# Layout of the query planes in DRAM, and their loads and stores, in the wide attention units of an encoder layer

## Chip, cores, metric

One core of one Trainium2 chip. The metric is the device time of one execution in microseconds; the median of three runs of the kernel before is 2199.79 us (2197.37 to 2203.7).

## The reference

One encoder layer is applied to two sequences with the same weights, A of 1024 positions (x_prompt) and B of 512 (x_sample). After an RMS norm one projection gives the inputs of an mLSTM branch, of a dilated window attention and of gates; both branches are projected, gated, merged, projected again, normed and added to x. What matters here is the attention: three groups (window, dilation) of eight heads of 64 channels each.

```
A_PATTERNS = ((128, 1), (512, 4), (2048, 16))
qr = ...residue(q)...       # positions regrouped by (position mod dilation)
logits = jnp.einsum('bghnqe,bghnke->bghnqk', qr, kb) + bias[:, None]
logits = jnp.where(mask, logits, -jnp.inf)
p = jnp.exp(logits - mx[..., None])
o = jnp.einsum('bghnqk,bghnke->bghnqe', p, vb)
```

q is scaled by 64 ** -0.5; the three groups' outputs are mixed by their softmax denominators. All is float32.

## The kernel before

**Numbers in two parts.** A float32 product is made of three TensorE passes over values that are split into a rounded part (hi) and the rest (lo): `mm3`, L209. So a tensor that TensorE reads is stored in DRAM as two planes.

**Stages.** First the input projection of A is made two output units of 128 channels at a time (`unit_pair`, L703; the pair stage). The weights of a pair (pw_raw) are loaded on SP (L692), split on ScalarE and VectorE (`pair_split`, tiles phla and phlb), and used from there. The first twelve pairs are the queries and keys of the attention; `att_unit` (L770) scales them, orders them by residue, splits them into hi and lo (tiles pwk, four buffers; ScalarE at L792, VectorE at L794) and stores both planes with `put` (L218), on SP (L222), into the DRAM tensor aqk_a. In this part of the program a scheduler sets the order on all engines but TensorE's. Then come, with TensorE's and SP's order as the program is written: the mLSTM of A, the attention of A, the mLSTM of B, the attention of B, the output stages. Beside each of them runs a queue of dense products (`Fill`): among them the projections of B, whose queries and keys go the same way into aqk_b, from the tiles sw (four buffers), as stores that are put off by some rounds (`put`, `tick`, `flush`, L218 to L239).

**Attention.** A unit u is two heads of a group (64 channels each, so 128 rows); u = 4 * group + pair, twelve units a sequence. A unit is wide if a residue's subsequence is longer than 128: units 0 to 7 of A, 0 to 3 of B. A wide unit has L1689's products: for each head hh the scores are two matmuls with the query tile `q[hh]` of 128 rows, against `k[hh]` (rows: the head's hi keys twice) and against `k[2 + hh]` (the head's lo keys in its own half of the rows, zeros in the other). For that, rows of `q[0]` are head 0's hi queries and, below, its lo queries; `q[1]` has head 1's lo above and its hi below:

```
for hh, rows in enumerate((A, B)):
    self.queue(("att", u), ("aqk", S, u), q[rows, hh].bitcast(F32), qd[0, rows])
    self.queue(("att", u), ("aqk", S, u), q[(B, A)[hh], hh].bitcast(F32), qd[1, rows])
    other = (B, A)[hh]
    for i, to in ((0, A), (0, B), (1, rows)):
        self.queue(("att", u), ("aqk", S, u + 12), kk[i][to, hh].bitcast(F32), kd[i, rows])
```

A is rows 0 to 63, B 64 to 127, `qd` the query planes, `kd` the key planes. So a wide unit has ten loads of 64 rows: four of queries (tile Q), six of keys (tiles V0a and V0b for an even unit, V1a and V1b for an odd one; in B V0a or V1a alone). Units with even pair number add loads of values (tile K, from av_a; X in B).

**What sets the order of the loads.** `att_load` (L1484) does not issue its loads, it queues them (L241). The next unit's loads are queued in the second round of a unit (`ready`, L1847), in A behind the two loads of its bias table. `spread` (L244) divides their number by the rounds left, rounded up, and `tick` (L234) issues that many in each round, on SP; what is left when a unit begins is issued then (`need`, L1879). In the same rounds SP issues the stores that have come due (og_a: the attention's outputs; vs_b and av_b: values of B from the tiles sw), each of which waits in order until its tile is written; the loads behind it wait too. For unit 0 of A the queue is spread over the last rounds of the mLSTM (L1454).

Of the kernel before, what the change touches and what calls it, by code (L numbers as in the profile page):

```python
# [29 lines left out]
P = 128  # L30
# [43 lines left out]
class Tokens:  # L74


    def __init__(self, dram, S, x, y, name):
        self.S, self.x, self.y, self.n, self.nblk, self.name = S, x, y, S // P, S // BLK, name
        t = lambda shape, what, dt=F32: dram.tile(shape, dt, name=f"{what}_{name}")
        self.qk = t([16, P, S], "qk")  # L80
        self.vs = t([2, S, D], "vs")
        self.G = t([8, P, S], "G")
        self.aqk = t([2, 24, P, S], "aqk")
        self.av = t([S, 1536], "av")
        self.az = t([4, P, S], "az")
        self.gt = t([2, 8, P, S], "gt")
        self.rw = t([8, self.n, 2, P], "rw")
        self.ym = t([12, P, S], "ym")
        self.og = t([S, 3, 4, OW], "og")


# [92 lines left out]
class Net:  # L184
# [585 lines left out]
    def att_unit(self, j, c, T, w):  # L770
# [3 lines left out]
        if g == 2:  # L774
            x = w()
            nc.scalar.activation(x.rearrange("p (r i) -> p r i", i=64), c.rearrange("p (i r) -> p r i", i=64), AF.Copy,
                                 scale=1.0 if keys else 0.125)
            self.put(("aqk", T.S, j), T.aqk[0, j], x, x)
            return
# [13 lines left out]
        for h, l, x in parts:  # L793
            nc.vector.scalar_tensor_tensor(l, x, 1.0 if keys else 0.125, h.bitcast(F32), op0=OP.mult, op1=OP.subtract)  # L794
        self.put(("aqk", T.S, j), T.aqk[0, j], hi.bitcast(F32), hi)
        self.put(("aqk", T.S, j), T.aqk[1, j], lo.bitcast(F32), lo)

# [686 lines left out]
    def att_load(self, T, u):  # L1484
# [25 lines left out]
        v = v.rearrange("p (n c) -> p n c", c=256)  # L1510
        qd, kd = T.aqk[:, u], T.aqk[:, u + 12]
        if wide:
            kk = self.narrow.get((T, "wide", u % 2)) or [x.rearrange("p (h s) -> p h s", h=2) for x in keys()]
            for hh, rows in enumerate((A, B)):
                self.queue(("att", u), ("aqk", S, u), q[rows, hh].bitcast(F32), qd[0, rows])
                self.queue(("att", u), ("aqk", S, u), q[(B, A)[hh], hh].bitcast(F32), qd[1, rows])
                other = (B, A)[hh]
                for i, to in ((0, A), (0, B), (1, rows)):
                    self.queue(("att", u), ("aqk", S, u + 12), kk[i][to, hh].bitcast(F32), kd[i, rows])
                if (T, "wide", u % 2) not in self.narrow:  # L1520
                    self.zeros.append(lambda x=kk[1][other, hh]: nc.gpsimd.memset(x.bitcast(F32), 0.0))
            self.narrow[T, "wide", u % 2] = kk
            k = [x[:, hh] for x in kk for hh in range(2)]
        else:
# [3 lines left out]
            k = self.narrow[T, u % 2]  # L1528
            self.queue(("att", u), ("aqk", S, u), q.bitcast(F32), qd.rearrange("a p s -> p a s"))
            for side, rows in enumerate((A, B)):  # L1530
                for i in range(2):
                    if new:
                        nc.gpsimd.memset(k[i][rows, :, 1 - side].bitcast(F32), 0.0)
                    self.queue(("att", u), ("aqk", S, u + 12), k[i][rows, :, side].bitcast(F32), kd[i, rows].rearrange("p (n s) -> p n s", s=P))
        if pr % 2 == 0:
# [7 lines left out]
    def compact_load(self, T, u):  # L1543
# [9 lines left out]
        if new:  # L1553
            self.queued += self.values_of(T, u, v)
        self.queue(("att", u), ("aqk", S, u), q, T.aqk[0, u])
        for hh in range(2):
            rows = slice(64 * hh, 64 * hh + 64)
            for z in (k, v) if new else ():
                nc.gpsimd.memset(z[rows, 1 - hh], 0.0)
            self.queue(("att", u), ("aqk", S, u + 12), k[rows, hh], T.aqk[0, u + 12, rows])  # L1560
        return q, k, v
# [940 lines left out]
```

## Time and profile before

| | |
|---|---|
| median of three runs | 2199.79 us (2197.37 to 2203.7) |
| the profiled execution | 2196.68 us |
| its span, from the first to the last instruction | 2194.8 us |
| mean granted clock of TensorE | 0.999 |
| HBM read, written | 274.70 MB, 113.44 MB |
| queue q1 (all that SP issues) | 276.15 MB, 40.5% of 16 engines |
| score matmuls of A's wide units (L1695) | start from 1305.9 to about 1497 us of the span |

PE is TensorE's matmuls, PEld its weight loads (they run beside matmuls), DVE VectorE, ACT ScalarE, POOL GpSimd, SP SyncE; SPq is SP's queue of DMA issues. In a row of the timeline stand start, duration, engine, line, operation, output<-input and, in brackets, the idle time before it with what ended it. A row of waits has the total, the times and the longest. Names have no buffer numbers: Q<-aqk_a is every query load of A. The time of an issue on SP is not that of the transfer; "to landing" is from the issue to the last byte's arrival.

### The profile page before, as it was taken

How to read it: one execution, taken by the hardware profiler on the slowest of the kernel's cores; microseconds unless marked ns; L12 is line 12 of the kernel's file. 1: busy time of each engine (PE TensorE's matmuls, PEld its weight loads, DVE VectorE, ACT ScalarE, POOL GpSimd, SP SyncE). 2: the span in 40 equal slices, each digit the busy share in tenths (PEclk: the TensorE clock that was granted, in tenths of full speed). 3: DMA queues.
4: the chain of work that ended last, by engine and by line, in shares of the span. 5: the costliest groups of instructions: out<-in, count | busy, mean ns of one | idle time of the engine just before them, and what ended most of it. 6: DMA issues, size and time to landing. Idle time of an engine off the chain costs nothing.

```text
span 2194.8 us, 34409 instructions
## 1 busy us (share of the span) xinstructions
PE 2180.1 (99%) x11962; PEld 1883.1 (86%) x11962; DVE 1460.9 (67%) x2970; ACT 1088.8 (50%) x2246; POOL 706.5 (32%) x994
## 2 busy tenths in 40 slices
PE   9999999999999999999999999999999999999998
PEld 8999888888888888888888889999788888888887
DVE  7775565657787555547888765574667855666673
ACT  7332243344444333446777656666755544554332
POOL 1000432333333222326776650011045522232331
PEclk9999999999999999999999999999999999999999
DMA  3842443433333222366646569997678786776772
GB/s 126 196 116 80 154 165 135 173 106 112 109 115 109 75 86 96 135 217 239 211 155 228 147 191 248 246 244 198 197 238 279 240 282 209 232 258 183 237 244 106
DMA packets 207640, 390.42 MB, mean 178 GB/s; under 512 B 37513, under 2 KB 121161, under 8 KB 207466
## 3 DMA queue, kind: packets, MB, share of 16 engines
q1 hardware_dynamic: 176584, 276.15, 40.5%
q0 software_dynamic: 27280, 99.48, 14.2%
q10 hardware_dynamic: 3602, 12.59, 1.4%
q8 instruction: 95, 1.56, 0.3%
q14 instruction: 79, 0.65, 0.1%
HBM read 274.70 MB, written 113.44 MB: 177 GB/s over the span
## 4 chain that ended last, share of the span: by engine, by line
PE 90%; DMA 4%; DVE 2%; issue 1%; ACT 1%; POOL 1%; SPq 0%; DVEq 0%; POOLq 0%; ACTq 0%
PE d L214 14%; PE d L212 14%; PE d L213 14%; PE dense L212 11%; PE dense L214 11%; PE dense L213 11%; PE lg L1695 1%; PE pt L1725 1%; PE num L212 1%; PE num L214 1%; PE num L213 1%; PE o L1768 1%; PE num L1390 1%; PE a L1097 1%; PE kv L212 1%
## 5 line engine op out<-in xcount | busy, mean ns | idle before, releaser
L212 PE MATMUL dense<-H,wh 128*128 128x512 f32 x664 | 269.4, 406 | 0.0
L213 PE MATMUL dense<-H,wh 128*128 128x512 f32 x664 | 260.4, 392 | 0.0
L214 PE MATMUL dense<-H,wl 128*128 128x512 f32 x664 | 260.3, 392 | 0.0
L213 PE MATMUL d<-Hl,phla 128*128 128x512 f32 x608 | 236.5, 389 | 0.0
L214 PE MATMUL d<-Hh,phla 128*128 128x512 f32 x608 | 236.5, 389 | 0.0
L212 PE MATMUL d<-Hh,phla 128*128 128x512 f32 x608 | 236.5, 389 | 0.0
L281 DVE TENSOR_TENSOR wl<-wraw,wh 128x1024 fp32r<-128x1024 f32 (+1 forms) x121 | 150.1, 1241 | 49.3 <-ACT wh L275 49.0
L214 PE MATMUL d<-Hh,phlb 128*128 128x512 f32 x456 | 177.4, 389 | 0.0
L212 PE MATMUL d<-Hh,phlb 128*128 128x512 f32 x456 | 177.4, 389 | 0.0
L213 PE MATMUL d<-Hl,phlb 128*128 128x512 f32 x456 | 177.4, 389 | 0.0
L275 ACT ACTIVATE wh<-wraw 128x1024 fp32r<-128x1024 f32 (+1 forms) x124 | 128.2, 1035 | 65.6 <-PE dense L213 21.9
L214 PEld LDWEIGHTS dense<-H,wl 128*128 128x128 f32 x664 | 124.7, 188 | 28.1
L697 POOL TENSOR_TENSOR psum_w<-pw_raw 128x512 f32<-128x512 f32 x38 | 55.3, 1455 | 283.3 <-DMA pw_raw<-w_in 266.0
L214 PE MATMUL d<-vhi,Hl 128*128 128x322 f32 x448 | 140.5, 314 | 0.5 <-DVE Hl L432 0.3
L212 PE MATMUL d<-vhi,Hh 128*128 128x322 f32 x448 | 140.3, 313 | 0.1
L213 PE MATMUL d<-vlo,Hh 128*128 128x322 f32 x448 | 139.6, 312 | 0.0
L212 PEld LDWEIGHTS dense<-H,wh 128*128 128x128 f32 x664 | 125.1, 188 | 16.5 <-issue 1.2
L213 PEld LDWEIGHTS dense<-H,wh 128*128 128x128 f32 x664 | 125.3, 189 | 14.7
L1714 DVE CUSTOM_DVE_ANT_0 ls<-lg,bias 128x256 f32<-128x256 f32 (+2 forms) x240 | 78.8, 352 | 85.5 <-PE lg L1695 63.7
L212 PEld LDWEIGHTS d<-Hh,phla 128*128 128x128 f32 x608 | 114.1, 188 | 23.7
L213 PEld LDWEIGHTS d<-Hl,phla 128*128 128x128 f32 x608 | 114.1, 188 | 23.7
L214 PEld LDWEIGHTS d<-Hh,phla 128*128 128x128 f32 x608 | 114.1, 188 | 23.6
(635 smaller groups left out, 5811.1 us busy)
## 6 DMA issues: line engine op xcount, KB each, us to landing
pw_raw<-w_in SPq DMA_DIRECT2D x76, 512.0 KB, 4.3
wraw<-w_in SPq DMA_DIRECT2D x63, 512.0 KB, 4.3
aqk_a<-pwk SPq DMA_DIRECT2D x40, 512.0 KB, 3.5
wraw<-w_pm POOLq DMA_DIRECT2D x24, 512.0 KB, 5.5
wraw<-w_out POOLq DMA_DIRECT2D x24, 512.0 KB, 4.0
aqk_b<-sw SPq DMA_DIRECT2D x40, 256.0 KB, 6.2
wraw<-w_v POOLq DMA_DIRECT2D x22, 430.0 KB, 7.2
qk_a<-pwk SPq DMA_DIRECT2D x16, 512.0 KB, 2.6
```

Source lines behind the costliest of these rows:

```text
L212: nc.tensor.matmul(out, lh, rh, start=start, stop=False, **kw)
L213: nc.tensor.matmul(out, lh, rl, start=False, stop=False, **kw)
L214: nc.tensor.matmul(out, ll, rh, start=False, stop=stop, **kw)
L275: high = nc.scalar.activation(hi[:, :n], raw[:, :n], AF.Copy)
L281: low = (self.lows or nc.vector).tensor_sub(lo[:, :n], raw[:, :n], hi[:, :n].bitcast(F32))
L697: self.nc.gpsimd.tensor_add(s[:, 0], ws[1][:, 0], ws[1][:, 1])
L1097: nc.tensor.matmul(p[:, c - c0], kT[:, ct, c * P:(c + 1) * P], qT[:, ct, c * P:(c + 1) * P], start=ct == 0, stop=ct == 1)
L1390: nc.tensor.matmul(pn, hi[:, j], z[:, c1], start=j == 0 and z is v[0], stop=False)
L1695: nc.tensor.matmul(lg[:, hh], q[hh][:, qs], z.rearrange("p (n j) -> p n j", j=P)[:, pair], start=z is k[hh], stop=z is not k[hh])
L1714: nc.vector.tensor_tensor_reduce(out=ls[rows, hh], in0=ts["lg"][hh][rows, of], in1=bt[rows, hh, by], scale=1.0, scalar=NEG, op0=OP.add, op ...
L1725: nc.tensor.transpose(pp[:, hh * nk + x], ts["ls"][:, hh, x * P:(x + 1) * P], self.ident)
L1768: nc.tensor.matmul(of(hh, 0, P), vh(kt[x], hh), pt[:, hh * len(kt) + x], start=x == 0, stop=x == len(kt) - 1)
```

## The change

The DRAM tensor aqk has, for each unit, four pieces of 64 rows instead of two planes of 128 rows. For keys, and for queries of units that aren't wide, `plane(j, i)` views two pieces as one plane, stored and loaded as before (the narrow units' loads and the six key loads are written for the new indices alone). Queries of wide units are stored in four pieces, in the order in which the tile wants them: head 0's hi, head 0's lo, head 1's lo, head 1's hi. Then `q[0]` and `q[1]` are each one load of 128 rows. A query store of 512 KB in A (256 KB in B) is two of half the size, and two query loads of 256 KB in A (128 KB in B) are one of twice the size. The six key loads of a wide unit stand in another order: the four of the hi keys with their head's queries, the two of the lo keys last. Bytes, tiles and arithmetic are the same.

```diff
--- before.py
+++ after.py
@@ -80,13 +80,19 @@
         self.qk = t([16, P, S], "qk")
         self.vs = t([2, S, D], "vs")
         self.G = t([8, P, S], "G")
-        self.aqk = t([2, 24, P, S], "aqk")
+        self.aqk = t([24, 4, 64, S], "aqk")
         self.av = t([S, 1536], "av")
         self.az = t([4, P, S], "az")
         self.gt = t([2, 8, P, S], "gt")
         self.rw = t([8, self.n, 2, P], "rw")
         self.ym = t([12, P, S], "ym")
         self.og = t([S, 3, 4, OW], "og")
+
+    def wide(self, g):
+        return self.S // min(DILS[g], self.n) > P
+
+    def plane(self, j, i):
+        return self.aqk[j, 2 * i:2 * i + 2].rearrange("a p s -> (a p) s")
 
 
 class Rot:
@@ -775,7 +781,7 @@
             x = w()
             nc.scalar.activation(x.rearrange("p (r i) -> p r i", i=64), c.rearrange("p (i r) -> p r i", i=64), AF.Copy,
                                  scale=1.0 if keys else 0.125)
-            self.put(("aqk", T.S, j), T.aqk[0, j], x, x)
+            self.put(("aqk", T.S, j), T.plane(j, 0), x, x)
             return
         dil = min(DILS[g], S // P)
         hi, lo = w(F32R), w(F32R)
@@ -792,8 +798,13 @@
             nc.scalar.activation(h, x, AF.Copy, scale=1.0 if keys else 0.125)
         for h, l, x in parts:
             nc.vector.scalar_tensor_tensor(l, x, 1.0 if keys else 0.125, h.bitcast(F32), op0=OP.mult, op1=OP.subtract)
-        self.put(("aqk", T.S, j), T.aqk[0, j], hi.bitcast(F32), hi)
-        self.put(("aqk", T.S, j), T.aqk[1, j], lo.bitcast(F32), lo)
+        if not keys and T.wide(g):
+            for x, slots in ((hi, (0, 3)), (lo, (1, 2))):
+                for i, to in enumerate(slots):
+                    self.put(("aqk", T.S, j), T.aqk[j, to], x[64 * i:64 * i + 64].bitcast(F32), x)
+        else:
+            for i, x in enumerate((hi, lo)):
+                self.put(("aqk", T.S, j), T.plane(j, i), x.bitcast(F32), x)
 
 
     def short_input(self, ps, xt):
@@ -1508,17 +1519,17 @@
             keys = lambda: [self.take(f"V{u % 2}{x}") for x in "ab"]
         q = q.rearrange("p (a s) -> p a s", a=2)
         v = v.rearrange("p (n c) -> p n c", c=256)
-        qd, kd = T.aqk[:, u], T.aqk[:, u + 12]
         if wide:
+            qd, kd = T.aqk[u], T.aqk[u + 12]
             kk = self.narrow.get((T, "wide", u % 2)) or [x.rearrange("p (h s) -> p h s", h=2) for x in keys()]
+            for hh in range(2):
+                self.queue(("att", u), ("aqk", S, u), q[:, hh].bitcast(F32), qd[2 * hh:2 * hh + 2].rearrange("a p s -> (a p) s"))
+                for to in (A, B):
+                    self.queue(("att", u), ("aqk", S, u + 12), kk[0][to, hh].bitcast(F32), kd[hh])
             for hh, rows in enumerate((A, B)):
-                self.queue(("att", u), ("aqk", S, u), q[rows, hh].bitcast(F32), qd[0, rows])
-                self.queue(("att", u), ("aqk", S, u), q[(B, A)[hh], hh].bitcast(F32), qd[1, rows])
-                other = (B, A)[hh]
-                for i, to in ((0, A), (0, B), (1, rows)):
-                    self.queue(("att", u), ("aqk", S, u + 12), kk[i][to, hh].bitcast(F32), kd[i, rows])
+                self.queue(("att", u), ("aqk", S, u + 12), kk[1][rows, hh].bitcast(F32), kd[2 + hh])
                 if (T, "wide", u % 2) not in self.narrow:
-                    self.zeros.append(lambda x=kk[1][other, hh]: nc.gpsimd.memset(x.bitcast(F32), 0.0))
+                    self.zeros.append(lambda x=kk[1][(B, A)[hh], hh]: nc.gpsimd.memset(x.bitcast(F32), 0.0))
             self.narrow[T, "wide", u % 2] = kk
             k = [x[:, hh] for x in kk for hh in range(2)]
         else:
@@ -1526,12 +1537,12 @@
             if new:
                 self.narrow[T, u % 2] = [x.rearrange("p (n b s) -> p n b s", n=n, b=2) for x in keys()]
             k = self.narrow[T, u % 2]
-            self.queue(("att", u), ("aqk", S, u), q.bitcast(F32), qd.rearrange("a p s -> p a s"))
+            self.queue(("att", u), ("aqk", S, u), q.bitcast(F32), T.aqk[u].rearrange("(a h) p s -> (h p) a s", a=2))
             for side, rows in enumerate((A, B)):
                 for i in range(2):
                     if new:
                         nc.gpsimd.memset(k[i][rows, :, 1 - side].bitcast(F32), 0.0)
-                    self.queue(("att", u), ("aqk", S, u + 12), k[i][rows, :, side].bitcast(F32), kd[i, rows].rearrange("p (n s) -> p n s", s=P))
+                    self.queue(("att", u), ("aqk", S, u + 12), k[i][rows, :, side].bitcast(F32), T.aqk[u + 12, 2 * i + side].rearrange("p (n s) -> p n s", s=P))
         if pr % 2 == 0:
             c0 = 512 * g + 256 * (pr // 2)
             x = S // dil // P
@@ -1552,12 +1563,12 @@
         k, v = self.narrow[T, "compact", u % 2]
         if new:
             self.queued += self.values_of(T, u, v)
-        self.queue(("att", u), ("aqk", S, u), q, T.aqk[0, u])
+        self.queue(("att", u), ("aqk", S, u), q, T.plane(u, 0))
         for hh in range(2):
             rows = slice(64 * hh, 64 * hh + 64)
             for z in (k, v) if new else ():
                 nc.gpsimd.memset(z[rows, 1 - hh], 0.0)
-            self.queue(("att", u), ("aqk", S, u + 12), k[rows, hh], T.aqk[0, u + 12, rows])
+            self.queue(("att", u), ("aqk", S, u + 12), k[rows, hh], T.aqk[u + 12, hh])
         return q, k, v
 
     def values_of(self, T, u, v):
```

No instruction of TensorE is moved; VectorE, ScalarE and GpSimd have a few neighbours exchanged. SP's order changes at these places. (Lines of the changed kernel are up to 11 higher: L222 and L228 become L228 and L234, L253 becomes L259, L692 becomes L698.)

SP in the pair stage, the first four pairs of queries, before:

```order
L692 DMA pw_raw<-w_in 128x1024
L2304 DMA av_a<-u2b 128x322 x2
L692 DMA pw_raw<-w_in 128x1024 x3
L222 DMA aqk_a<-pwk 128x1024 x4
L692 DMA pw_raw<-w_in 128x1024 x2
L222 DMA aqk_a<-pwk 128x1024 x4
L692 DMA pw_raw<-w_in 128x1024 x2
L222 DMA aqk_a<-pwk 128x1024 x4
L692 DMA pw_raw<-w_in 128x1024 x2
```

The same place of the changed kernel:

```order
L698 DMA pw_raw<-w_in 128x1024
L2315 DMA av_a<-u2b 128x322 x2
L698 DMA pw_raw<-w_in 128x1024 x3
L228 DMA aqk_a<-pwk 64x1024 x8
L698 DMA pw_raw<-w_in 128x1024 x2
L228 DMA aqk_a<-pwk 64x1024 x8
L698 DMA pw_raw<-w_in 128x1024 x2
L228 DMA aqk_a<-pwk 64x1024 x8
L698 DMA pw_raw<-w_in 128x1024 x2
```

Each group of four stores of 128 rows (two units, hi and lo) has become eight of 64 rows, at the same place among the weights' loads.

SP in the attention of A, the loads of unit 3, before, from behind the loads of its bias table, with the stores that stand between them (ot is a tile of attention outputs):

```order
L253 DMA Q_13028<-aqk_a 64x1024 x2
L228 DMA og_a<-ot_12421 128x4x132
L228 DMA vs_b<-sw_7815 128x414
L228 DMA vs_b<-sw_7816 128x414
L253 DMA V1a<-aqk_a 64x1024 x2
L253 DMA V1b<-aqk_a 64x1024
L253 DMA Q_13028<-aqk_a 64x1024 x2
L253 DMA V1a<-aqk_a 64x1024
L228 DMA vs_b<-sw_7817 128x430
L228 DMA vs_b<-sw_7814 128x430
L253 DMA V1a<-aqk_a 64x1024
L253 DMA V1b<-aqk_a 64x1024
```

The same loads in the changed kernel:

```order
L259 DMA Q_13046<-aqk_a 128x1024
L259 DMA V1a<-aqk_a 64x1024
L234 DMA og_a<-ot_12443 128x4x132
L234 DMA vs_b<-sw_7831 128x414
L234 DMA vs_b<-sw_7832 128x414
L259 DMA V1a<-aqk_a 64x1024
L259 DMA Q_13046<-aqk_a 128x1024
L259 DMA V1a<-aqk_a 64x1024 x2
L259 DMA V1b<-aqk_a 64x1024 x2
L234 DMA vs_b<-sw_7833 128x430
L234 DMA vs_b<-sw_7830 128x430
```

The last two loads before, one each of V1a and V1b, stood behind the second pair of vs_b stores that is shown; now all six key loads and both query loads stand ahead of it.

SP in the attention of A, the loads of unit 6, before:

```order
L253 DMA bias_12410<-erow 128x256 x2
L253 DMA Q_13957<-aqk_a 64x1024 x2
L253 DMA V0a<-aqk_a 64x1024 x2
L228 DMA og_a<-ot_12419 128x2x132
L228 DMA og_a<-ot_12419 64x2x132 x2
L228 DMA vs_b<-sw_7814 128x180
L228 DMA vs_b<-sw_7815 128x180
L228 DMA av_b<-sw_7816 128x250
L253 DMA V0b<-aqk_a 64x1024
L253 DMA Q_13957<-aqk_a 64x1024 x2
L253 DMA V0a<-aqk_a 64x1024 x2
L253 DMA V0b<-aqk_a 64x1024
```

The same loads in the changed kernel:

```order
L259 DMA bias_12432<-erow 128x256 x2
L259 DMA Q_13969<-aqk_a 128x1024
L259 DMA V0a<-aqk_a 64x1024 x2
L259 DMA Q_13969<-aqk_a 128x1024
L234 DMA og_a<-ot_12441 128x2x132
L234 DMA og_a<-ot_12441 64x2x132 x2
L234 DMA vs_b<-sw_7830 128x180
L234 DMA vs_b<-sw_7831 128x180
L234 DMA av_b<-sw_7832 128x250
L259 DMA V0a<-aqk_a 64x1024 x2
L259 DMA V0b<-aqk_a 64x1024 x2
L259 DMA K_13968<-av_a 128x2x256 x4
```

All that the query tile needs now stands ahead of the stores; behind them are four loads of keys instead of six of keys and queries, the last V0b again the last of them.

## The prediction

> **What bounds the kernel now.** I read the page first, then the table of stretches, the waits of TensorE, its timeline where a wait is named, and the SP queue beside it.
>
> ```profile
> span 2194.8 us, 34409 instructions
> PE 2180.1 (99%) x11962; PEld 1883.1 (86%) x11962; DVE 1460.9 (67%) x2970; ACT 1088.8 (50%) x2246; POOL 706.5 (32%) x994
> DMA  3842443433333222366646569997678786776772
> ```
>
> TensorE is busy for all of the span but 14.7 us. The last row has one digit for each fortieth of the span; the three nines from 1317 to 1482 us are the wide attention units of A, the stage with the fullest DMA engines. The table of stretches (start and end; length; busy time of each engine; granted clock; DMA share; GB/s) shows what TensorE loses in each stage that the change touches: the pair stage with A's stores, the mLSTM of A with B's stores, the wide units of A, those of B.
>
> ```profile
> 200.00:960.00 760.00, 760.00 (x3441) 635.53 (x3440) 488.46 (x544) 299.24 (x313) 239.78 (x203) 1.00 0.34 119
> 960.00:1250.00 290.00, 290.00 (x1743) 256.64 (x1742) 228.30 (x448) 202.50 (x478) 185.31 (x293) 1.00 0.64 207
> 1310.00:1510.00 200.00, 199.08 (x1600) 185.88 (x1599) 122.59 (x508) 130.28 (x389) 21.14 (x33) 1.00 0.91 238
> 1790.00:1925.00 135.00, 134.56 (x735) 115.74 (x735) 83.09 (x225) 72.15 (x189) 32.96 (x63) 1.00 0.73 229
> ```
>
> Where A's and B's stores are made, TensorE loses nothing. In A's wide units it loses 0.92 us with the DMA engines 91% full, in B's 0.44 us. The waits of TensorE (in total, times, longest) say on what; two are for tensors that the change touches, and they are these.
>
> ```profile
> PE lg L1695 <- DMA V0b<-aqk_a: 0.4, 1, 0.4
> PE lg L1695 <- DMA V1b<-aqk_a: 0.2, 1, 0.2
> ```
>
> A busy matmul's end is modelled, so I take the price of a wait from starts, not ends. This is TensorE at the first tile of unit 3, then of unit 6:
>
> ```profile
> 1379.34 0.28 PE L1695 MATMUL lg<-V1a,Q 128*128 128x256 f32 x1
> 1379.45 0.28 PE L1695 MATMUL lg<-V1b,Q 128*128 128x256 f32 x1
> 1379.73 0.38 PE L1695 MATMUL lg<-V1a,Q 128*128 128x256 f32 x1
> 1380.36 0.39 PE L1695 MATMUL lg<-V1b,Q 128*128 128x256 f32 x1 [0.25 <-DMA V1b<-aqk_a]
> ```
> ```profile
> 1452.23 0.28 PE L1695 MATMUL lg<-V0b,Q 128*128 128x256 f32 x1
> 1452.35 0.28 PE L1695 MATMUL lg<-V0a,Q 128*128 128x256 f32 x1
> 1453.02 0.39 PE L1695 MATMUL lg<-V0b,Q 128*128 128x256 f32 x1 [0.40 <-DMA V0b<-aqk_a]
> ```
>
> Two such matmuls start 0.12 us apart when nothing is late. In unit 3 the steps are 0.28 and 0.63, so 0.16 + 0.51 = 0.67 us are lost; in unit 6 one step is 0.67, so 0.55 us. **All that the loads of these tensors cost the kernel today is 1.22 us.**
>
> **The change part by part.** *Loads.* Eight wide units of A and four of B give up four query loads of 64 partitions for two of 128: 24 fewer on SP. *Stores.* The same twelve query units store four pieces instead of two: 24 more. Issue times on SP (min/median/max ns), from the rows of the stores in the pair stage and of the loads in A's attention:
>
> ```profile
> L222 SPq DMA_DIRECT2D aqk_a<-pwk x40: 319/326/2290, 256.3 to 468.6; - x40
> L253 SPq DMA_DIRECT2D Q<-aqk_a x30: 444/594/2192, 1310.6 to 1505.5; - x30
> ```
>
> SP gives up 24 x 0.594 = 14.3 us and takes on 24 x 0.326 = 7.8 us. Neither is on TensorE's path by itself; what counts is when a transfer lands.
>
> How fast a transfer moves is bounded by two stretches, one of 128-row stores and a 128-row load, one of 64-row loads alone beside the weights' loads:
>
> ```profile
> 276.00:283.00 7.00, 7.00 (x32) 5.79 (x32) 2.86 (x5) 2.11 (x5) 3.83 (x3) 1.00 0.82 330
> 1314.00:1326.00 12.00, 12.00 (x84) 10.65 (x85) 7.89 (x27) 7.96 (x22) 1.09 (x2) 1.00 0.99 243
> ```
>
> Full engines move 330 / 0.82 = 402 GB/s in the first, 243 / 0.99 = 245 GB/s in the second. 512 KB (524,288 bytes) then take 1.30 us as one transfer of 128 rows and 2.14 us as two of 64. If the whole difference is due to the rows, a merged load saves 0.84 us, 1.7 us for a unit; if it is due to the crowd in that stretch, nothing. I take the upper end, since both stretches are made of 4 KB rows, and keep the lower.
> [...]
>
> *Unit 3's wait.* The chain that ended last has the two late loads with their time to landing, and the SP queue shows why the first was late:
>
> ```profile
> 1372.44 7.87 DMA V1b<-aqk_a
> 1443.69 9.29 DMA V0b<-aqk_a
> ```
> ```profile
> 1365.61 1.23 SPq L253 DMA_DIRECT2D V1a<-aqk_a  x1
> 1370.64 1.24 SPq L228 DMA_DIRECT2D vs_b<-sw  x2
> 1371.94 0.45 SPq L253 DMA_DIRECT2D V1a<-aqk_a  x1
> 1372.44 0.59 SPq L253 DMA_DIRECT2D V1b<-aqk_a  x1
> ```
>
> The load stood behind two stores that SP could not issue before 1370.64, and landed at 1380.31. In the new order both V1b loads stand ahead of those stores (second pair of order rows): six loads stand there now as before, and before they were all issued by 1366.84 (first row). The last then lands, with the 7.87 or 9.29 us of the late ones, by 1374.7 or 1376.1, over 3 us before TensorE reads it at 1379.45. The 0.67 us go.
>
> *Unit 6's wait.* Here the order around the stores stays, but ahead of the last V0b stand two loads fewer:
>
> ```profile
> 1438.07 3.39 SPq L253 DMA_DIRECT2D Q<-aqk_a  x2
> 1443.69 0.45 SPq L253 DMA_DIRECT2D V0b<-aqk_a  x1
> ```
>
> SP is held up here by its full queue (3.39 us for two issues of 0.44), and the second query load now goes out before the stores of 1431 to 1436 instead of in this jam. The load has to land 0.55 us sooner; 1.7 us of transfer less gives that, and 0 us would not. The 0.55 us go, with less certainty.
>
> *The tightest of the others.* Unit 5's last keys are just in time (two SP rows, the times to landing of these four loads, and TensorE's first use of V1b):
>
> ```profile
> 1419.12 0.45 SPq L253 DMA_DIRECT2D Q<-aqk_a  x1
> 1420.90 0.59 SPq L253 DMA_DIRECT2D V1b<-aqk_a  x1
> ```
> ```profile
> DMA to landing us min/median/max: 5.7/6.1/7.0
> ```
> ```profile
> 1428.45 0.28 PE L1695 MATMUL lg<-V1b,Q 128*128 128x256 f32 x1
> ```
>
> The last load lands at 1427.9 at the latest, 0.55 us before it is read. The first V1b load moves from 1414.98 (before a group of stores) to behind it, where the query load stood, and the second follows it: about 1419.1 and 1419.7, the last 1.2 us earlier than now. No wait is added. Unit 2's queue goes from 13 loads at three a round to 11 at two: only its value load moves behind a pair of stores, and it is used three rounds after the scores.
>
> *The stores of A.* In the pair stage each of four pairs gets four more stores:
>
> ```profile
> 256.25 3.92 SPq L222 DMA_DIRECT2D aqk_a<-pwk  x4
> 271.92 1.57 SPq L692 DMA_DIRECT2D pw_raw<-w_in  x2
> 275.29 3.02 SPq L222 DMA_DIRECT2D aqk_a<-pwk  x4
> ```
> ```profile
> SPq L692 <- POOL psum_w L715: 407.2, 36, 17.4
> ```
>
> Behind the stores SP holds the next weights' loads, which wait for GpSimd anyway: from 260.17 to 271.92 SP is idle, 11.75 us, and 4 x 0.326 = 1.3 us fall into that. Without that cover it would be 4 x 1.3 = 5.2 us. The engines are 41% to 82% busy there; four planes at 0.84 us more are 3.4 us of the 19.04 us between pairs. The buffers come free later, though. ScalarE's next use of them is this:
>
> ```profile
> 255.22 2.05 ACT L792 ACTIVATE pwk<-c 128x960 fp32r<-128x960 f32 x3
> 263.67 0.24 ACT L792 ACTIVATE pwk<-c 128x64 fp32r<-128x64 f32 x1
> 268.09 1.06 ACT L678 ACTIVATE phla<-psum_w 128x1024 fp32r<-128x1024 f32 x1 [4.18 <-PE d L214]
> ```
> ```profile
> DMA to landing us min/median/max: 2.6/3.5/6.9
> ```
>
> The first plane's second half is issued at about 256.6 and lands, with the median of these stores and 0.84 us, at about 261, and with the longest 6.9 at 263.5, before 263.67. Behind that instruction ScalarE has 4.18 us of idle before the next weights. I take nothing.
>
> *The stores of B* put two more issues, 0.65 us, ahead of a weight load in each of four units, in a stretch where TensorE is busy 290.00 of 290.00 us; without cover 4 x 0.65 = 2.6 us. I take nothing.
>
> **Sum.** 2196.68 us (the profiled execution: its span and 1.88 us around it) - 0.67 - 0.55 = 2195.46 us. The median of the runs is 3.11 us above that execution, so I forecast 2195.46 + 3.11 = **2198.6 us**, 0.05% less. A measurement of this kernel can tell about 0.3% from no change, 6.6 us: this is no change.
>
> **The rivals.**
> *The waits stay, or another unit's take their place.* The bytes are the same and the queue is full; if 64 rows are no slower, unit 6 stays late and a later first key load shows in unit 5. For it: unit 5's margin of 0.55 us. Against: the order at unit 3. At most the two waits and as much again: 2199.8 to 2201.0 us. Also no change.
> *TensorE waits inside its busy time, and faster by over 0.3%.* In A's wide units the weight loads are busy for 185.88 of 200 us; were the missing 14.1 us time lost to loads, the change could give 2199.8 - 14.1 = 2185.7 us.
> Against: between 200 and 960 us (first row of the table of stretches) the weight loads are busy for 635.53 us of 760, 84%, and TensorE waits for nothing at all, so a missing share is no wait.
> [...]
> *Slower by over 0.3%: the split stores hold ScalarE.* Place: the pair stage, four times. A half plane that lands later than 263.67 + 4.18 = 267.85, so over 11.3 us after its issue, delays the next weights' split, and TensorE with it, by as much as it is late; from 13 us on (1.65 us late, four times 6.6 us) it is 2206.4 us or more. For it: half the rows, a slower transfer. Against: the longest landing in that stage is 6.9 us.
>
> **How the numbers follow.** Waits gone: 0.62. Waits stay or move: 0.27. Faster by over 0.3%: 0.05, half of it the rival, half the spread of medians (the runs of before lie between 2197.37 and 2203.7). Slower by over 0.3%: 0.06 in the same way. Within 0.3%: 0.89. The first two cases lie between 2198.6 and 2201.0; with the spread of the runs, 2.4 us below and 3.9 us above their median, and a further 2 us below for a median that falls nearer the profiled execution, I give 2194.2 to 2204.9.
>
> **What would show it.** TensorE's waits without V0b and V1b of aqk_a; the first four lg matmuls of units 3 and 6 0.12 us apart; query loads of 512 KB landing in about the time of today's 256 KB; DMA share of the stretch of A's wide units below 0.91; 760.00 of 760.00 us busy in the pair stage. It would be wrong if a wait for pwk shows on ScalarE, if a first lg matmul of another unit waits for its keys, or if the busy time itself changes.

## The result, and the profile after

| | before | after |
|---|---|---|
| median of seven runs | 2199.79 us (2197.37 to 2203.7) | 2193.68 us (2192.12 to 2195.6) |
| the profiled execution | 2196.68 us, below all seven runs | 2195.6 us, the slowest of the seven |
| its span | 2194.8 us | 2193.8 us |

The ratio is 0.9971, with a 95% interval of 0.9961 to 0.9981: faster by 6.1 us, where 1.2 us were forecast; the median lies 0.5 us under the range that was given (2194.2 to 2204.9). The two profiled executions differ by only 1.1 us. Most of the gain is therefore in no comparison of these two traces, and that is the subject of this study.

The page of the changed kernel (its line numbers are 6 to 11 higher: L1695 is L1706 now, L253 is L259, L222 is L228):

```profile
PE 2179.9 (99%) x11962; PEld 1883.7 (86%) x11962; DVE 1463.6 (67%) x2970; ACT 1089.6 (50%) x2246; POOL 709.8 (32%) x994
DMA  3842453433333222367646559897678786776773
```

The busy times are those of before, to 0.2 us for TensorE; of the three nines in the DMA row two are left. The four stretches of the prediction:

```profile
200.00:960.00 760.00, 760.00 (x3439) 635.53 (x3438) 491.57 (x543) 299.28 (x311) 242.22 (x199) 1.00 0.35 119
960.00:1250.00 290.00, 290.00 (x1747) 256.81 (x1746) 228.67 (x450) 202.74 (x477) 183.96 (x297) 1.00 0.64 209
1310.00:1510.00 200.00, 199.87 (x1608) 187.30 (x1608) 123.52 (x513) 131.06 (x394) 20.69 (x33) 1.00 0.88 239
1790.00:1925.00 135.00, 135.00 (x739) 116.71 (x738) 84.58 (x227) 74.25 (x195) 34.27 (x64) 1.00 0.74 234
```

TensorE still loses nothing where the stores are made (first two rows). In A's wide units the DMA share is 0.88 instead of 0.91, and TensorE loses 0.13 us instead of 0.92; in B's it loses nothing instead of 0.44 us. The waits of TensorE from 1310 to 1930 us are these, and none is for a tensor that the change touches:

```profile
PE num L1401 <- ACT X L1411: 0.7, 1, 0.7
PE sc L220 <- DVE kl L1332: 0.4, 1, 0.4
```

TensorE's timeline at the first tile of unit 3 and of unit 6:

```profile
1379.50 0.28 PE L1706 MATMUL lg<-V1a,Q 128*128 128x256 f32 x1
1379.62 0.28 PE L1706 MATMUL lg<-V1b,Q 128*128 128x256 f32 x1
1379.73 0.28 PE L1706 MATMUL lg<-V1a,Q 128*128 128x256 f32 x1
1379.86 0.29 PE L1706 MATMUL lg<-V1b,Q 128*128 128x256 f32 x1
```
```profile
1451.51 0.28 PE L1706 MATMUL lg<-V0a,Q 128*128 128x256 f32 x1
1451.62 0.28 PE L1706 MATMUL lg<-V0b,Q 128*128 128x256 f32 x1
1451.74 0.28 PE L1706 MATMUL lg<-V0a,Q 128*128 128x256 f32 x1
1452.15 0.39 PE L1706 MATMUL lg<-V0b,Q 128*128 128x256 f32 x1
```

Unit 3 runs at 0.12 us a step, as forecast. In unit 6 one step is still 0.41 us, 0.29 too much, without a wait in brackets: by the chain that ended last, the last load of V0b was issued at 1442.26 and took 9.85 us, so it landed at 1452.11, just before the matmul at 1452.15. In the second execution of the same kernel, told below, these matmuls start 0.12 us apart.

The transfers, with KB each and the median time to landing:

```profile
aqk_a<-pwk SPq DMA_DIRECT2D x24, 512.0 KB, 3.3
Q<-aqk_a SPq DMA_DIRECT2D x20, 512.0 KB, 6.3
aqk_a<-pwk SPq DMA_DIRECT2D x32, 256.0 KB, 3.9
```

A query load of 512 KB lands in 6.3 us, where one of 256 KB over 64 rows took 6.6 before (7.1 against 6.1 in the second traces of the two kernels): twice the bytes in about the same time. The same bytes also take less of the DMA engines. These are the rows of SP's queue from 1310 to 1510 us (packets, MB, share of 16 engines), before and after:

```profile
q1 hardware_dynamic: 29685, 36.68, 72.6%
q1 hardware_dynamic: 29654, 36.73, 69.1%
```

That is 7.0 us less of the 200, for 14 merged pairs of query loads some 0.5 us a pair (an estimate from these two rows). The prediction's bounds were 0 and 0.84 us.

The price is there too: a store of half a plane lands in 3.9 us, one of a whole plane in 3.3. What ScalarE does after such stores is a small lesson in reading a releaser. Its waits at the place that the prediction named, second pair, before and after:

```profile
281.74 1.06 ACT L678 ACTIVATE phla<-pw_raw 128x1024 fp32r<-128x1024 f32 x1 [4.89 <-PE d L214]
```
```profile
282.51 1.06 ACT L684 ACTIVATE phla<-pw_raw 128x1024 fp32r<-128x1024 f32 x1 [4.89 <-DMA aqk_a<-pwk]
```

The name of the releaser has changed, the idle time has not: 4.89 us in both. The store now lands last by the profile, but ScalarE starts no later in its step than it did, and TensorE waits for nothing there: it costs nothing.

### The profile page after: what moved, and what is told of

It reads as the page before. It is cut to its first block, busy times and chain, and to the rows that moved or that the text cites. A ratio compares the mean times of both kernels' runs of the same rounds, so it can differ in the third digit from the quotient of the medians.

```text
span 2193.8 us, 34390 instructions
## 1 busy us (share of the span) xinstructions
PE 2179.9 (99%) x11962; PEld 1883.7 (86%) x11962; DVE 1463.6 (67%) x2970; ACT 1089.6 (50%) x2246; POOL 709.8 (32%) x994
## 4 chain that ended last, share of the span: by engine, by line
PE 93%; DMA 2%; DVE 2%; issue 1%; ACT 1%; POOL 1%; DVEq 0%; SPq 0%; POOLq 0%; ACTq 0%
PE d L220 14%; PE d L218 14%; PE d L219 14%; PE dense L218 12%; PE dense L220 12%; PE dense L219 12%; PE lg L1706 2%; PE pt L1736 1%; PE num L218 1%; PE num L220 1%; PE num L219 1%; PE o L1779 1%; PE o L1758 1%; PE a L1108 1%; PE num L1401 1%
```

## The experiments

Twelve kernels ran, in three groups; the kernels of a group and the kernel before ran on one chip. All ratios are to before, with 95% intervals, and a gain in us without another word is by the ratio, which can differ from the difference of the medians by about 1 us. Before's median in the three groups was 2199.72, 2200.8 and 2199.74 us.

Beside the ratio I use one number of each trace, the time from the first score matmul of A's unit 0 to that of unit 7, and the same from B's unit 0 to its unit 3. These are the four rows for before:

```profile
1305.85 0.37 PE L1695 MATMUL lg<-V0a,Q 128*128 128x256 f32 x1
1476.45 0.28 PE L1695 MATMUL lg<-V1a,Q 128*128 128x256 f32 x1
1779.51 0.64 PE L1695 MATMUL lg<-V0a,Q 128*128 128x256 f32 x4
1846.11 0.61 PE L1695 MATMUL lg<-V1a,Q 128*128 128x256 f32 x3
```

That is 170.60 us for A and 66.60 us for B. The least that any trace shows is 168.42 us (three traces) and 66.10 us (five); above that is time lost, whatever TensorE waited for. Of the 2.18 us that A lies above the least here, 1.22 are the waits for late keys that the prediction priced; 0.7 are at unit 0, where TensorE's named wait is for ScalarE (pt at 1311.19). Outside these stretches the traces differ too, by 2.1 us ahead of A, 1.8 between the two and 4.1 behind B.

### The kernel before, profiled once more

No edit. 

> The kernel before, unchanged, to see how its waits differ from one execution to another. The first trace lost 1.2 us to late loads of aqk_a (units 3 and 6), while the median of the runs lay 3.1 us above that execution. Theory Q (the query loads of the wide units are what makes keys late, in a different unit each time): this trace shows more than 1.2 us of first score matmuls waiting for aqk_a, 3 to 6 us if its time is near 2200 us. Theory S (the time went elsewhere, to stages that the change touches only by chance): at a time near 2200 us the waits for aqk_a are again about 1 us and the excess is in other stages. Ratio to the kernel before 1.000 by both, within 0.1%.

Measured: 0.9999 (0.9986 to 1.0011), median 2199.32; the profiled execution took 2205.71 us. The same four rows:

```profile
1306.68 0.37 PE L1695 MATMUL lg<-V0a,Q 128*128 128x256 f32 x1
1480.52 0.28 PE L1695 MATMUL lg<-V1a,Q 128*128 128x256 f32 x1
1783.52 0.64 PE L1695 MATMUL lg<-V0a,Q 128*128 128x256 f32 x4
1853.56 0.61 PE L1695 MATMUL lg<-V1a,Q 128*128 128x256 f32 x3
```

A: 173.84 us, 5.42 above the least, where the first trace had 2.18. B: 70.04 us, 3.94 above, where it had 0.50. TensorE's timeline at unit 6 shows how a wait of half a microsecond became several:

```profile
1451.80 0.28 PE L1695 MATMUL lg<-V0a,Q 128*128 128x256 f32 x1
1451.92 0.28 PE L1695 MATMUL lg<-V0b,Q 128*128 128x256 f32 x1
1454.41 0.38 PE L1695 MATMUL lg<-V0a,Q 128*128 128x256 f32 x1 [2.21 <-DMA V0a<-aqk_a]
1455.56 0.39 PE L1695 MATMUL lg<-V0b,Q 128*128 128x256 f32 x1 [0.76 <-DMA V0b<-aqk_a]
1456.43 0.55 PE L213 MATMUL dense<-X,H 128*128 128x430 f32 x1
1456.77 0.56 PE L214 MATMUL dense<-X,H 128*128 128x430 f32 x1
1457.13 0.56 PE L212 MATMUL dense<-X,H 128*128 128x430 f32 x1
1459.28 0.41 PE L1695 MATMUL lg<-V0a,Q 128*128 128x256 f32 x1
```

Two steps of the scores are 2.49 and 1.15 us instead of 0.12: 3.40 us lost. Then the dense matmuls start 0.36 us apart instead of 0.20, for some eight of them. The second tile of scores (last row) starts 7.48 us after the first, where 2.68 is the least of all traces: 4.80 us lost, of which 1.40 are these slower matmuls, and no row calls that a wait. The table of stretches says why (the granted clock is the third number from the right):

```profile
1450.00:1456.00 6.00, 3.02 (x17) 2.56 (x16) 2.48 (x13) 2.04 (x7) 0.00 (x0) 1.00 1.04 269
1456.00:1459.00 3.00, 3.00 (x13) 2.80 (x12) 1.46 (x6) 1.09 (x4) 0.00 (x0) 0.57 0.77 222
1459.00:1465.00 6.00, 6.00 (x50) 5.59 (x50) 3.78 (x16) 2.91 (x8) 0.18 (x1) 0.93 0.98 236
```

The first row has TensorE idle for 3 of 6 us with the DMA engines full (a share of 1.04), the second a clock of 0.57. The last of the late loads is the same V0b as in the first trace, issued at nearly the same time; its landing differs, 12.20 us after the issue instead of 9.29 (chain that ended last):

```profile
1443.32 12.20 DMA V0b<-aqk_a
```

B's loss stands at another place, which the prediction did not count to these loads: the products that run between the first scores of B's unit 1 and those of unit 2.

```profile
1818.14 0.39 PE L214 MATMUL dense<-K,wl 128*128 128x512 f32 x1
1819.35 0.50 PE L212 MATMUL dense<-K,wh 128*128 128x512 f32 x1 [0.82 <-ACT K L2045]
1820.67 0.50 PE L213 MATMUL dense<-K,wh 128*128 128x512 f32 x1 [0.82 <-DVE K L2046]
```
```profile
1805.23 9.66 DMA sraw<-ym_a
```

Their operand K is split on ScalarE and VectorE from rows of ym_a, which GpSimd's queue loads; the chain that ended last leads back to such a load that took 9.66 us to land. Behind the two waits the matmuls are slower here too: from 1821.73 to 1823.44 us they start 0.43 us apart, where it was 0.23 ahead of the waits.

That B's query loads made this load late is not shown. Where B's query loads have 128 rows, ScalarE's order is another one at this very place. These are its rows in this trace, then in that of the changed kernel:

```profile
1814.90 0.63 ACT L2045 ACTIVATE K<-sraw 128x512 fp32r<-128x512 f32 x1 [0.64 <-DMA sraw<-ym_a]
1816.42 1.05 ACT L275 ACTIVATE Q<-wraw 128x1024 fp32r<-128x1024 f32 x1
```
```profile
1809.76 1.04 ACT L281 ACTIVATE Q<-wraw 128x1024 fp32r<-128x1024 f32 x1
1811.19 0.62 ACT L2056 ACTIVATE K<-sraw 128x512 fp32r<-128x512 f32 x1
```

Before, the split of the rows of ym_a stands ahead of two exponentials of the attention and of the split of weights (Q<-wraw), so that ScalarE waits 0.64 us for the load ahead of them; after, it stands behind them. The seven traces with query loads of 128 rows in B all have this exchange, and the seven with B's loads as before all have the old order; in A's attention ScalarE, VectorE and GpSimd have the same order in all fourteen. So in B the loads and the exchange can't be told apart.

So what TensorE waits differs from one execution to the next, and the first trace was a lucky one.

### The stores alone

Layout and stores as after, the loads as before (four of 64 rows, old order):

```
for hh, rows in enumerate((A, B)):
    for i, to in enumerate((A, B) if hh == 0 else (B, A)):
        self.queue(..., q[to, hh].bitcast(F32), qd[2 * hh + (i if hh == 0 else 1 - i)])
    ...
```

> The changed kernel's DRAM layout and its four stores of 64 rows, but the loads as before: four query loads of 64 rows a unit, in the old order. Theory Q: no gain, 2199 to 2201 us, since the loads are what counts and the stores lie under cover. Theory P (the split stores or the layout bring the gain): 2193 to 2195 us.

Measured: 1.0006 (0.9996 to 1.0016), median 2202.47. The split stores cost nothing that can be told from no change, and at most 3.5 us by the interval's upper end. A's stretch is 171.65 us: the waits of before are still there, so the gain is not in the stores or the layout.

### The merged loads with the old order of keys

```
-            for hh in range(2):
+            for hh, rows in enumerate((A, B)):
                 ...
-            for hh, rows in enumerate((A, B)):
                 self.queue(..., kk[1][rows, hh].bitcast(F32), kd[2 + hh])
```

> The changed kernel with merged query loads, but the key loads in the old order (each head's lo keys right behind its hi keys). Theory Q: all of the gain, 2193 to 2195 us. Theory O (the gain is from the order, the lo keys last): 2197 to 2200 us.

Measured: 0.9977 (0.9968 to 0.9986), median 2195.48. The merged loads bring four fifths of the gain (0.23% of 0.29%) without the new order of the keys; whether the order adds the rest (1 to 2 us) is inside the intervals. Between this kernel and the stores alone nothing but the query loads is edited, and their medians lie 7.0 us apart (2202.47 and 2195.48); B's exchanged order on ScalarE is in that difference. Its profiled execution, the slowest of its twelve, has a long stall at unit 6 (two rows of TensorE's timeline, and the stretch behind it):

```profile
1454.15 0.35 PE L1705 MATMUL lg<-V0a,Q 128*128 128x256 f32 x1 [1.70 <-DMA av_b<-sw]
1455.23 0.39 PE L1705 MATMUL lg<-V0b,Q 128*128 128x256 f32 x1 [0.72 <-DMA V0b<-aqk_a]
```
```profile
1456.00:1459.00 3.00, 3.00 (x20) 2.91 (x19) 1.75 (x10) 1.48 (x5) 0.00 (x0) 1.00 0.72 177
```

After this stall the clock stays at 1.00 and nothing is slowed. With the old order of keys unit 6 can still be late, then, with merged loads too. (The first row's releaser is named as a store, though the matmul reads V0a and Q.)

### The change for A alone

`if not keys and T.wide(g) and T.n > 4` at the stores, and the same condition at the loads; B as before. 

> The change for A alone; B's wide units store two planes and load four pieces of 64 rows, as before. Theory Q, in A's attention with its full DMA engines: 2193 to 2195 us, nearly all of the gain. If B's attention gives the most: 2197 to 2199 us.

Measured: 0.9983 (0.9973 to 0.9992), median 2196.74: 3.7 us, some 60% of the gain (3.0 us between the medians). A's stretch is 168.51 us, B's 67.11.

### The order of the keys alone

The kernel before with the two loads of lo keys last:

```
+                for to in (A, B):
+                    self.queue(..., kk[0][to, hh].bitcast(F32), kd[0, rows])
+            for hh, rows in enumerate((A, B)):
-                for i, to in ((0, A), (0, B), (1, rows)):
-                    self.queue(..., kk[i][to, hh].bitcast(F32), kd[i, rows])
+                self.queue(..., kk[1][rows, hh].bitcast(F32), kd[1, rows])
```

> The kernel before with nothing but the changed kernel's order of the key loads: both heads' hi keys first, the lo keys last; four query loads of 64 rows as before. Theory R (128 rows move faster, so the last keys of unit 6 and the loads beside B's units come sooner): no gain, 2198 to 2201 us. Theory O (the order): 2194 to 2197 us.

Measured: 0.9985 (0.9977 to 0.9994), median 2197.64. Some 3 us, which I cannot place: its one trace has A's stretch at 172.41 us, no better than before's, with waits of 1.6 us for V0b and a granted clock of 0.61 behind them (1456 to 1459 us). Before's median is 1.1 us higher in this group than in the other two, so a part of the 3 us may be chance.

### As many loads as before, but of 128 rows

```
-                self.queue(..., q[:, hh].bitcast(F32), qd[2 * hh:2 * hh + 2].rearrange("a p s -> (a p) s"))
+                for x in (slice(0, S // 2), slice(S // 2, S)):
+                    self.queue(..., q[:, hh, x].bitcast(F32), qd[2 * hh:2 * hh + 2, :, x].rearrange("a p s -> (a p) s"))
```

> The changed kernel's layout and stores, but each query tile in two loads of 128 rows and half the columns: as many loads as before and as many bytes each, all rows at once. Theory R (rows): most of the gain stays, 2193 to 2196 us. Theory N (the number of loads in SP's queue): the gain goes, 2198 to 2200 us.

Measured: 0.9971 (0.9961 to 0.9982), median 2195.58; the whole gain, with four query loads a unit as before. The number of issues is thus not the cause. The nearest kernel is the order of the keys alone: its ten loads of a unit stand in the same places of the queue, but its query loads have 64 rows, of 4 KB instead of 2. It has 0.9985, and the medians lie 2.1 us apart. From 1310 to 1510 us SP's queue takes 68.8% of 16 engines here (36.75 MB) and 72.6% there (36.34 MB), and A's stretch is 168.89 against 172.41 us. That points to the rows; B's exchanged order is in the 2.1 us as well.

### Unit 6 alone

`j == 6` and `u == 6` added to the conditions of A alone. 

> The change for unit 6 of A alone; the other eleven wide units store and load as before. Theory U (the wait of unit 6 is the one that varies, up to 2.9 us with 1.3 us of slower matmuls behind it): 2196 to 2198 us, more than half of what the change for A alone gave (3.7 us), and no wait for V0b of aqk_a near 1453 us. Theory W (waits of many units, each a little): less than 1 us of gain, 2199 to 2200 us.

Measured: 0.9986 (0.9977 to 0.9994), median 2197.63: 3.1 us, so most of A's 3.7 may come from this one unit, though the two intervals (1.3 to 5.1 and 1.8 to 5.9 us) are wide. No instruction of ScalarE, VectorE or GpSimd is exchanged in this kernel: by its trace, their order is that of before. In its trace the first two tiles of unit 6 start 2.68 us apart, the least that any trace has; before had 3.35 and 7.48.

### Unit 6's loads earlier, nothing else

The kernel before, with these loads spread over four rounds instead of six:

```
-self.spread(T.n - (2 if T.n > 4 else 1) if i or T.n > 4 else 1)
+self.spread(T.n - (2 if T.n > 4 else 1) - (2 if T.n > 4 and i == 5 else 0) if i or T.n > 4 else 1)
```

> The kernel before with unit 6's loads in four rounds instead of six: two more 64-row loads stand ahead of the stores that hold SP up, the rest behind them as before. Theory U with the queue's position as the cause: as much gain as the change for unit 6 alone, 2196 to 2198 us. If the rate of 64 rows is the cause, unit 6's last key load is late as before: 2198 to 2200 us.

Measured: 0.9986 (0.9977 to 0.9995), median 2198.28. With loads of 64 rows throughout, this brings as much as the change does at this unit, though in its one trace unit 6 still loses 0.71 us. The last V0b itself is not issued sooner there (at 1444.42, against 1443.69 and 1443.32 in the traces of before); fewer loads stand between the stores and it, and it lands in 8.60 us. So wider transfers and loads moved ahead both help at this unit; that it is by the landing of V0b fits the waits, and is not shown for the runs without a trace.

### The change again, for B alone, and two attempts to go further

The changed kernel once more: 

> The changed kernel, unchanged, for a second trace of it. Theory V (the loads of 64 rows cost a different amount in each execution, at unit 6 of A and at the output products near 1815 us that run beside B's units; merged, they cost little in all): both places again lose under 0.5 us together, no matmuls slowed behind them, ratio 0.997. If the first trace of the changed kernel was a lucky one: over 1 us at one of the two.

Measured: 0.9974 (0.9965 to 0.9983), median 2194.06. A's stretch is 168.42 us, B's 66.10, the least in both. The runs fit a wait that varies and is gone: these ten lie between 2192.37 and 2195.97 us, before's 33 in this group between 2195.36 and 2205.8.

The change for B alone (`T.n <= 4` in the conditions): 

> The change for B alone. Theory V: unit 6 of A loses 0.5 to 5 us as before, the output products near 1815 us lose nothing; the time falls by what is left of the whole gain beside that for A alone (6.1 - 3.7 = 2.4 us): ratio 0.9985 to 0.9993. If the gain for A alone was all there is: 0.9995 to 1.0005.

Measured: 0.9996 (0.9986 to 1.0005), median 2198.38; 0.9 us, and no gain that the runs can tell, less than expected. Its trace does have B's stretch at 66.10 us, though the load of ym_a at that place takes 10.8 us to land, longer than the 9.66 above: it is not by a faster load that B loses nothing here. A's loss is as before (172.62 us), with these waits at unit 6:

```profile
PE lg L1714 <- DMA V0a<-aqk_a: 0.8, 1, 0.8
PE lg L1714 <- DMA V0b<-aqk_a: 0.8, 1, 0.8
```

The changed kernel with unit 6's loads earlier too (the edit above): 

> The changed kernel with unit 6's loads in four rounds instead of five, one more key load ahead of the stores. Theory V: unit 6's wait, 0.3 us in the changed kernel's trace, goes; ratio 0.9970, no different from the changed kernel within what can be measured. If unit 6 still costs the changed kernel some us in its other executions: 0.995 to 0.996.

Measured: 0.9978 (0.997 to 0.9987), median 2194.66, no different from the change without it. Its trace has A at the least, 168.42 us: unit 6 has no loss left that this could take. B's stretch is 66.99 us here.

The changed kernel with the hi keys stored twice, so that their four loads of 64 rows are two of 128:

```
+        elif T.wide(g):
+            for to in range(4):
+                i = to // 2
+                self.put(("aqk", T.S, j), T.aqk[j, to], hi[64 * i:64 * i + 64].bitcast(F32), hi)
...
-                for to in (A, B):
-                    self.queue(..., kk[0][to, hh].bitcast(F32), kd[hh])
+                self.queue(..., kk[0][:, hh].bitcast(F32), kd[2 * hh:2 * hh + 2].rearrange("a p s -> (a p) s"))
```

> The changed kernel with each head's hi keys of a wide unit kept twice in DRAM, one copy behind the other, so that two loads of 128 rows take the place of four of 64; a wide key unit has five stores instead of two. Theory V: the same means once more, where the waits it could remove are nearly gone: 0 to 1 us below the changed kernel, ratio 0.9966 to 0.9972. If the stages of the wide units are held up by the DMA engines all along: 3 us or more below it, ratio under 0.996.

Measured: 0.9981 (0.9972 to 0.9989), median 2194.6. A's wide units here, and in the second execution of the change:

```profile
1310.00:1510.00 200.00, 200.00 (x1612) 187.73 (x1611) 123.97 (x513) 130.73 (x392) 21.46 (x33) 1.00 0.80 239
```
```profile
1310.00:1510.00 200.00, 200.00 (x1612) 187.71 (x1611) 124.22 (x517) 131.26 (x393) 22.54 (x34) 1.00 0.88 240
```

The DMA share falls from 0.88 to 0.80, and TensorE is busy for 200.00 of 200 us in both: nothing waited here, and the freer engines brought nothing (medians of 2194.6 and 2194.06 us). No kernel of the study beats the changed one.

### All traces side by side

Time above the least, in us (A from 168.42, B from 66.10), grouped by how the loads of that sequence are made:

| loads as before | A | B | | loads as after | A | B |
|---|---|---|---|---|---|---|
| before | 2.18 | 0.50 | | after | 0.42 | 0.02 |
| before, again | 5.42 | 3.94 | | after, again | 0.00 | 0.00 |
| stores alone | 3.23 | 1.13 | | A alone | 0.09 | |
| B alone | 4.20 | | | B alone | | 0.00 |
| A alone | | 1.01 | | change, unit 6 earlier | | 0.89 |
| unit 6 alone | | 1.63 | | | | |
| unit 6 earlier | | 2.21 | | | | |
| mean | 3.76 | 1.74 | | mean | 0.17 | 0.23 |

By the means 3.6 us in A and 1.5 us in B, 5.1 together, against 6.1 and 5.7 us between the medians (change, and change again). Of A's 3.76 us 2.6 are the step from unit 6 to unit 7 (0.67, 5.05, 1.19 and 3.67); the rest is spread over units 0, 3, 4 and 5, and some of it names ScalarE. The kernels that change something else: the order of the keys alone 3.99 in A and 1.53 in B, unit 6 alone 0.59 in A, unit 6 earlier 1.21 without the change and 0.00 with it, loads by columns 0.47 and 0.00, hi keys twice 0.00 and 0.00. An exception is the merged loads with the old order of keys, 2.93 in A and 0.00 in B, in the slowest of its runs.

## Why the prediction was wrong, point by point

- **The step that failed: "All that the loads of these tensors cost the kernel today is 1.22 us."** In A the mechanism was right and the size was off. The 1.22 us are the waits of one execution, which was faster than any of the seven runs. In another execution of the same kernel the late loads cost 4.80 us at unit 6 alone, 1.40 of them as slowed matmuls; over the four traces with old loads A loses 3.76 us on average, 2.6 of them at unit 6, and the change for A alone brings 3.7 us in the runs. The rest of the 6.1 us is B's, below.
- **The offset.** "The median of the runs is 3.11 us above that execution" was added as a constant. Of the gain of 6.1 us only 1.1 lie between the two profiled executions; 5.0 are this offset, which is 3.1 us before and -1.9 after. So it was no constant: it held, for the most part, what a typical execution waits more than the lucky one. A part of it may be chance, since the changed kernel's profiled executions lay 1.9 us above its medians both times. From 2196.68 us to the median the sum should have asked which waits grow; the DMA share of 0.91 and margins of some tenths of a microsecond were the sign that they can.
- **"A measurement of this kernel can tell about 0.3% from no change"**: it told more: seven runs of each gave 0.29% with an interval from 0.19% to 0.39%.
- **B.** Its 0.44 us were seen in the table of stretches and not followed, since TensorE's wait there names ScalarE and VectorE and not aqk_b. Behind them stands a load of ym_a, whose split ScalarE has in another place since the change. The traces give 1.5 us; the runs give 0.9 us with B alone and 2.6 us between A alone and the whole change (0.9983 to 0.9971), with intervals that hold all of these. No run has B's loads of 128 rows with the old order on ScalarE, or the other way round, so the cause of this part stays open. The prediction named the exchanged neighbours nowhere in its sum or its rivals.
- **Unit 3.** Its wait is gone, but it was chance: of the traces with old loads in A, only the first (0.67 us) and the one of the stores alone (0.48 us) have it. The argument from the order of issues explained one sample.
- **Unit 6.** Right in place and in means. Unit 6 alone brings 3.1 us, and loads moved ahead bring as much. Left is a margin near zero (0.29 us late in one execution, none in the other).
- **The upper end for a load of 64 rows** (0.84 us saved by a merged one) was nearer than "nothing", but too high: the engines' share gives some 0.5 us a pair.
- **The stores** cost nothing, as forecast: 1.0006 with an interval to 1.0016, 760.00 of 760.00 us busy.
- **The rivals.** That waits stay or move: no; no wait for these tensors is named any more in the span of both sequences' attention. That TensorE loses time inside its busy time: not as proposed, the weight loads' share of A's wide units is 187 of 200 us after as well, with nothing waiting. But a part of the loss was inside busy time, as matmuls at a lower clock behind a stall (1.40 us at 0.57 and 0.93 in the second trace of before). That ScalarE is held by the stores: no, its idle time is the same 4.89 us.

Left open: what frees B's part; why the order of the keys alone brings some 3 us (0.9985), which its trace does not show; and why the gain by medians, 5.7 to 6.1 us, is a little above the 5.1 us of the traces. Six of the fourteen profiled executions were the slowest among the runs they were taken with, where chance would give about one, so a profiled execution may wait longer than a run without the profiler, and the traces may overstate the losses.

## What to carry to other kernels

A wait of half a microsecond in one profile, at a load that lands just in time on nearly full DMA engines, is a sample and not a price (here 0.55 us in one execution and 4.80 in another, at DMA shares of 0.91 and 0.90 in the stage): set the profiled execution beside the runs first, and if it lies at the edge of them, take a second trace before any wait is priced. The gap between the profiled execution and the median is then a term to be explained, since a change may remove just that. In this kernel late loads were helped by widening them to 128 rows (3.1 us for unit 6 alone, its keys in the new order) and by moving them ahead (3.1 us); where TensorE waited for nothing, neither brought anything (2194.6 and 2194.66 us, against 2194.06). And where a change exchanges neighbours on other engines, look where: here they stand at the very place of one of the two gains.

## What the runs showed of the hardware

- A stall of TensorE can cost more than its length. In the second trace of before two waits of 2.21 and 0.76 us, with one matmul between them, were followed by 3 us at a granted clock of 0.57 and 6 us at 0.93, which cost 1.40 us more. Shorter ones were followed by a lower clock too: 1.15 and 0.47 us by 0.61 from 1456 to 1459 us (order alone), 0.84 and 0.76 us by 0.74 in the same stretch (B alone). With the old order of keys and merged loads two waits of 1.70 and 0.72 us at the same place were followed by a clock of 1.00. So the length of the waits alone does not decide; what does, these traces don't show.
- The landing time of one and the same load differs between executions of one kernel by 2.9 us (9.29 and 12.20 us for the last V0b), with the issue 0.37 us apart.
